# The substitution of a block inversion on GpSimd instead of VectorE, with a planned delay of 41 in place of 36

## The chip, the cores and the metric

One core of a Trainium2 chip runs the whole program. The metric is the device time of one execution in microseconds (us); the kernel before has a median of 1866.65 us over three runs (1861.1 to 1870.76). The engines in this text: PE is TensorE (matmul), PEld its weight loads, DVE is VectorE, ACT is ScalarE, POOL is GpSimd, and SP is SyncE, which here only issues DMAs. Each engine works its own queue in order; semaphores tie the queues together.

## The reference

One decoder layer for a prompt of 1024 tokens and 8 samples of 8 tokens, width 1024. A normalized input goes through one wide projection; its columns feed a sliding-window attention (branch A) and an RWKV-7 recurrence (branch B); both branches are gated, projected, merged and projected once more. The change concerns branch B alone:

```python
def step(S, inp):
    rt, wt, kt, vt, at, bt = inp
    sa = jnp.einsum('bhvk,bhk->bhv', S, at)
    S = S * wt[:, :, None, :] + sa[..., None] * bt[:, :, None, :] + vt[..., None] * kt[:, :, None, :]
    return S, jnp.einsum('bhvk,bhk->bhv', S, rt)
```

This runs over the tokens for 16 heads of 64 by 64 state.

## The kernel before

The recurrence is not computed token by token. The tokens are cut into chunks of 64, and within a chunk the effect of the earlier tokens on the later ones is a triangular system whose matrix is inverted. Sixteen blocks, numbered s = 0 to 15, cover it: s is 4 times the head pair group p (0 to 3) plus the quarter q (0 to 3) of the sequence. A block holds eight such matrices (two pairs of heads, four chunks c), and each block with q = 3 has a second, smaller set for the samples. That makes 20 inversions.

A block goes through these steps. `prep` and `front` (L588) form the arrays and the score matrices: matmuls into PSUM tiles A, which ACT (L803) and DVE (L801) copy to `ab`. `invert` (L833) takes the diagonal blocks of 16 by 16: SP writes `ab` to DRAM (s1, L842) and reads it back with one small matrix per partition (TM, L848); then 15 steps of forward substitution follow, each a multiply into Tt (L854) and an addition into TR (L856), both of 8 to 36 elements per partition and each needing the one before; SP writes TR to DRAM (s2, L858). `merge` (L861) reads the inverses back into `dinv` (L875, half of it issued on SP and half on POOL), transposes them on DVE (L878) and joins the blocks to 64 by 64 by four groups of small matmuls on PE (tiles q_a to q_d). The result is `ti`. `chain` (L921) carries the state through the four chunks of the block. For each chunk: POOL prepares sp, the decayed state (L946); PE forms px; DVE copies it to xs (L954); PE applies ti (tile c, from xs and ti); DVE copies to vsu (L959); PE forms pn; DVE adds sp and pn to the next state in vsu (L970). The chain of block s starts from the state of block s − 1 and needs ti of block s, so the merge of a block must be done by the time that the chain of the block before it ends. `posts` normalizes and gates the output (POOL L1038, L1044, L1045, and the DMA of L1046).

What sets the order: on PE alone the order of this stage is written out by a planner, `drive` (L142). It keeps a clock of planned PE time (`clk`), to which every matmul adds a fixed cost, and eight streams: chains, merges, fronts, preps, samples, posts and the dense projections. A stream says with each `yield` from when it may go on, as a mark plus a delay. The merge of block s waits for the mark `f{s}`, set behind the scores and the inversion, plus WI (L865): the time that the plan allows for the way from the scores to dinv. Where no other stream is due, dense matmuls of the projections (tile d, with weights split into whi and wlo) fill in.

The queues of DVE, ACT, POOL and SP are ordered by a scheduler from priorities and its own estimates: chains and merges have 400000 (`CHAIN`), the inversions 150000 (`INV`, L609), the rest 200000 or 0. So the engine of an instruction also changes where others stand.

POOL has besides the splitting of the weights (L171, 128x1024), the token shift of the projections (L407, L414), the weight DMAs (L169) and the spill DMAs (L426).

Of the kernel before, what the change touches and what calls it, by code (L numbers as in the profile page):

```python
# [12 lines left out]
ALU = mybir.AluOpType  # L13
# [24 lines left out]
MAN = {mybir.EngineType.PE, mybir.EngineType.SP, mybir.EngineType.Pool}  # L38
WX = 0.06
YPR = (200000, 0, 0)  # L40
WI, WD, WB, WA, WM, WH, WS, WP, WT, WR, WE = 36.0, 5.0, 6.0, 2.5, 5.0, 2.0, 3.0, 6.0, 10.0, 4.0, 14.0


T_LORA = 0
# [37 lines left out]
class Prog:  # L82
# [750 lines left out]
    def invert(self, nm, ab, n0, nn):  # L833


        nc, ep = self.nc, self.ep
        nb = 8 * nn
        np_ = 2 * nb
        s1 = self.dp.tile([4 * nn, 32, 32], F32, name=f"s1{nm}")
        s2 = self.dp.tile([2, 4, nn, 16, 16], F32, name=f"s2{nm}")  # L840
        for g in range(4):
            nc.sync.dma_start(s1[g * nn:g * nn + nn].rearrange("n j t -> j n t"), ab[32 * g:32 * g + 32, n0:n0 + nn, 32 * (g % 2):32 * (g % 2) + 32])  # L842
        M = ep.tile([P, 16, 16], F32, tag="TM", name=f"TM{nm}", bufs=1)
        R = ep.tile([P, 8, 16], F32, tag="TR", name=f"TR{nm}", bufs=1)
        tmp = ep.tile([P, 64], F32, tag="Tt", name=f"Tt{nm}", bufs=1)
        for a in range(2):
            for k in range(2):
                nc.sync.dma_start(M[nb * a:nb * a + nb].rearrange("(b k) j t -> k b j t", k=2)[k], s1[:, 16 * a:16 * a + 16, 16 * a:16 * a + 16])  # L848
        nc.sync.dma_start(R[:np_], self.I["ri"][:np_].rearrange("p (a b) -> p a b", a=8))
        for s in range(15):  # L850
            w = 15 - s
            cc = s // 2 + 1
            tv = tmp[:np_, :cc * w].rearrange("p (c t) -> p c t", c=cc)
            nc.vector.tensor_tensor(tv, M[:np_, s:s + 1, s + 1:16].to_broadcast([np_, cc, w]),  # L854
                                    R[:np_, 0:cc, s:s + 1].to_broadcast([np_, cc, w]), ALU.mult)
            nc.vector.tensor_tensor(R[:np_, 0:cc, s + 1:16], R[:np_, 0:cc, s + 1:16], tv, ALU.add)  # L856
        for k in range(2):
            nc.sync.dma_start(s2.rearrange("a g n (c k) t -> k (a g n) c t", k=2)[k], R[:np_].rearrange("(b k) c t -> k b c t", k=2)[k])  # L858
        return s2
# [739 lines left out]
```

## Time and profile before

| | |
|---|---|
| median of 3 runs | 1866.65 us (1861.1 to 1870.76) |
| the profiled execution | 1864.38 us |
| its span | 1862.6 us |
| mean granted PE clock | 0.949 |
| busy: PE, DVE, ACT, POOL | 1686.4, 1139.5, 932.9, 618.0 us |
| stages | start 0 to 190, recurrence 190 to 1300, attention and output to 1863 us |

Busy times say how long an engine worked, not whether anyone waited for it. A wait in the trace is idle time of an engine, put down to what ended it. The granted clock is a share of PE's full speed: 1.00 is the upper of its two levels and 0.5 the lower, so a mean of 0.94 is a mixture of the two. "c" is the PSUM tile of the chain, "d" that of the dense projections.

### The profile page before, as it was taken

Reading aid. Unit: us, or ns where it says so; the run is one execution under the profiler, and the core shown is the slowest. Engines: PE = TensorE matmul, PEld = TensorE weight load, DVE = VectorE, ACT = ScalarE, POOL = GpSimd, SP = SyncE. Lnnn points to the kernel's source line nnn. Section 1 sums busy time; section 2 is a strip of 40 time slices with the busy share of each in tenths; the row PEclk is TensorE's granted clock in tenths of the full one; section 3 lists DMA queues with packets and bytes.
Section 4 is the critical chain, followed back from the end, with each engine's and each line's share of the span. In section 5 each row is a group of like instructions: output and inputs, shape, how many; then the busy total and the mean of one; then the engine's idle time right before and its main releaser. Section 6 shows DMA issues by size and latency. Waiting matters only on the chain. (4 is left out here: it accounts for less than half of the span.)

```text
span 1862.6 us, 37492 instructions
## 1 busy us (share of the span) xinstructions
PE 1686.4 (91%) x13792; PEld 1584.5 (85%) x13792; DVE 1139.5 (61%) x3224; ACT 932.9 (50%) x2353; POOL 618.0 (33%) x872
## 2 busy tenths in 40 slices
PE   5899889888888989889888899999999999999997
PEld 4799888887787878778888888899999899899997
DVE  5323667866777676787676578642366776544443
ACT  5444555444445556555545565434466765432233
POOL 5466444444442653445463343344200000000000
PEclk8899999898898999999999899999999999999999
DMA  4234433333333334334333343223612344364531
GB/s 159 103 126 128 110 97 95 99 97 88 90 97 103 103 93 115 99 101 112 91 105 97 102 136 89 73 90 101 196 60 66 122 130 149 114 221 133 181 109 60
DMA packets 233687, 206.90 MB, mean 111 GB/s; under 512 B 135904, under 2 KB 202608, under 8 KB 233472
## 3 DMA queue, kind: packets, MB, share of 16 engines
q1 hardware_dynamic: 214624, 149.33, 28.0%
q0 software_dynamic: 18880, 55.17, 9.3%
q8 instruction: 109, 1.79, 0.4%
q14 instruction: 74, 0.61, 0.1%
HBM read 140.42 MB, written 65.98 MB: 111 GB/s over the span
## 5 line engine op out<-in xcount | busy, mean ns | idle before, releaser
L110 PE MATMUL d<-hhi,whi 128*128 128x364 f32 (+1 forms) x1656 | 585.7, 354 | 28.6 <-ACT zz L406 9.5
L110 PE MATMUL d<-hlo,whi 128*128 128x364 f32 (+1 forms) x1656 | 568.2, 343 | 11.0 <-DVE hlo L352 8.3
L110 PEld LDWEIGHTS d<-hhi,whi 128*128 128x128 f32 x1656 | 329.6, 199 | 36.5 <-ACT zz L406 10.7
L110 PEld LDWEIGHTS d<-hlo,whi 128*128 128x128 f32 x1656 | 329.5, 199 | 21.0 <-DVE hlo L352 13.0
L110 PE MATMUL d<-hhi,wlo 128*128 128x364 f32 (+1 forms) x1656 | 340.7, 343 | 0.0
L110 PEld LDWEIGHTS d<-hhi,wlo 128*128 128x128 f32 x1656 | 286.5, 196 | 3.4 <-issue 2.4
L171 POOL TENSOR_TENSOR wlo<-wraw,whi 128x1024 fp32r<-128x1024 f32 x56 | 134.3, 2398 | 144.8 <-PE d L110 53.4
L170 ACT ACTIVATE whi<-wraw 128x1024 fp32r<-128x1024 f32 x90 | 94.9, 1055 | 72.8 <-PE d L110 50.7
L1434 POOL TENSOR_TENSOR xr<-xr,frs 128x256 f32<-128x256 f32 x2 | 1.8, 932 | 344.7 <-ACT frs L1431 344.7
L407 POOL TENSOR_TENSOR zz<-zz,pad 128x364 f32<-128x364 f32 (+1 forms) x75 | 71.9, 959 | 116.0 <-ACT pad L404 54.6
L946 POOL TENSOR_TENSOR sp<-vsu,pc 64x128 f32<-64x128 f32 x128 | 57.2, 446 | 125.1 <-DVE vsu L970 115.8
L970 DVE SCALAR_TENSOR_TENSOR vsu<-c,pc,sp 64x64 f32<-64x64 f32 x240 | 67.9, 283 | 41.1 <-PE c L110 37.9
L854 DVE TENSOR_TENSOR Tt<-TM,TR 128x30 f32<-128x30 f32 (+3 forms) x300 | 81.8, 273 | 17.6 <-DMA TM<-s 8.5
L856 DVE TENSOR_TENSOR TR<-TR,Tt 128x30 f32<-128x30 f32 (+3 forms) x300 | 87.3, 291 | 7.1
L1173 ACT ACTIVATE sc<-sc,st 128x256 f32<-128x256 f32 (+1 forms) x128 | 61.8, 484 | 24.5 <-DVE st L1169 24.4
L405 ACT ACTIVATE pad<-d,prm 128x364 f32<-128x364 f32 (+1 forms) x75 | 40.6, 541 | 57.4 <-PE d L110 57.1
L110 PE MATMUL c<-vsu,kbt 128*128 128x128 f32 x256 | 43.1, 292 | 26.0 <-DVE vsu L959 25.9
L1084 POOL TENSOR_TENSOR ylo<-ys,yhi 128x364 fp32r<-128x364 f32 (+1 forms) x6 | 6.5, 1078 | 178.0 <-ACT yhi L1083 178.0
L110 PE MATMUL d<-yhi,whi 128*128 128x364 f32 (+1 forms) x192 | 64.7, 337 | 0.6 <-DVE mb L1354 0.6
L110 PEld LDWEIGHTS c<-vsu,kbt 128*128 128x128 f32 x256 | 36.6, 196 | 33.4 <-DVE vsu L959 32.6
L110 PE MATMUL d<-ol,whi 128*128 128x364 f32 (+1 forms) x192 | 63.1, 329 | 1.5 <-DVE ol L230 1.5
L110 PE MATMUL d<-oh,whi 128*128 128x364 f32 (+1 forms) x192 | 63.3, 330 | 1.2 <-ACT oh L229 1.2
(362 smaller groups left out, 3883.5 us busy)
## 6 DMA issues: line engine op xcount, KB each, us to landing
wraw<-in_w POOLq DMA_DIRECT2D x56, 512.0 KB, 4.2
wraw<-in_w SPq DMA_DIRECT2D x37, 512.0 KB
d_z<-zz POOLq DMA_DIRECT2D x48, 182.0 KB, 2.4
zv<-d_z SPq DMA_DIRECT2D x48, 128.0 KB
w<-d_c SPq DMA_DIRECT2D x24, 256.0 KB
d_m<-sp SPq DMA_DIRECT2D x32, 182.0 KB
stageo<-d_o SPq DMA_DIRECT2D x8, 544.0 KB
d_z<-zz POOLq DMA_DIRECT2D x24, 180.0 KB, 3.8
```

The costliest lines, as they stand in the source:

```text
L110: self.nc.tensor.matmul(out, lhsT=lhsT, rhs=rhs, **kw)
L170: nc.scalar.activation(hi, raw, AF.Copy)
L171: (nc.vector if self.dve_lo else nc.gpsimd).tensor_tensor(lo, raw, hi.bitcast(F32), ALU.subtract)
L405: nc.scalar.activation(pad[:, 1:1 + m], ps[:, :m], AF.Copy, scale=mu)
L407: nc.gpsimd.tensor_tensor(z[:, :m], z[:, :m], pad[:, 0:m], ALU.add)
L854: nc.vector.tensor_tensor(tv, M[:np_, s:s + 1, s + 1:16].to_broadcast([np_, cc, w]), R[:np_, 0:cc, s:s + 1].to_broadcast([np_, cc, w]), AL ...
L856: nc.vector.tensor_tensor(R[:np_, 0:cc, s + 1:16], R[:np_, 0:cc, s + 1:16], tv, ALU.add)
L946: nc.gpsimd.tensor_tensor(sp[h], vsu[h, c, :, h], pc[h, c].unsqueeze(2).to_broadcast([64, 2, HD]), ALU.mult)
L970: nc.vector.scalar_tensor_tensor(dst, pn[h, i, h], pc[h, c, i:i + 1], sp[h, i], ALU.mult, ALU.add)
L1084: (self.nc.gpsimd if kt % 4 == 3 else self.nc.vector).tensor_tensor(lo, t, hi.bitcast(F32), ALU.subtract)
L1173: nc.scalar.activation(sc[k], sc[k], AF.Exp, bias=st[:, 0, k:k + 1], accum_out=st[:, 1, k:k + 1])
L1434: en.tensor_tensor(xt[:, dt, :n], xt[:, dt, :n], rst[:, :n], ALU.mult)
```

## The change

The two operations of each substitution step go from DVE's queue to POOL's, and WI from 36 to 41. Nothing is added or left out.

```diff
--- before.py
+++ after.py
@@ -38,7 +38,7 @@
 MAN = {mybir.EngineType.PE, mybir.EngineType.SP, mybir.EngineType.Pool}
 WX = 0.06
 YPR = (200000, 0, 0)
-WI, WD, WB, WA, WM, WH, WS, WP, WT, WR, WE = 36.0, 5.0, 6.0, 2.5, 5.0, 2.0, 3.0, 6.0, 10.0, 4.0, 14.0
+WI, WD, WB, WA, WM, WH, WS, WP, WT, WR, WE = 41.0, 5.0, 6.0, 2.5, 5.0, 2.0, 3.0, 6.0, 10.0, 4.0, 14.0
 
 
 T_LORA = 0
@@ -851,9 +851,9 @@
             w = 15 - s
             cc = s // 2 + 1
             tv = tmp[:np_, :cc * w].rearrange("p (c t) -> p c t", c=cc)
-            nc.vector.tensor_tensor(tv, M[:np_, s:s + 1, s + 1:16].to_broadcast([np_, cc, w]),
+            nc.gpsimd.tensor_tensor(tv, M[:np_, s:s + 1, s + 1:16].to_broadcast([np_, cc, w]),
                                     R[:np_, 0:cc, s:s + 1].to_broadcast([np_, cc, w]), ALU.mult)
-            nc.vector.tensor_tensor(R[:np_, 0:cc, s + 1:16], R[:np_, 0:cc, s + 1:16], tv, ALU.add)
+            nc.gpsimd.tensor_tensor(R[:np_, 0:cc, s + 1:16], R[:np_, 0:cc, s + 1:16], tv, ALU.add)
         for k in range(2):
             nc.sync.dma_start(s2.rearrange("a g n (c k) t -> k (a g n) c t", k=2)[k], R[:np_].rearrange("(b k) c t -> k b c t", k=2)[k])
         return s2
```

What follows are pieces of the queues at block 8 (pair 2, quarter 0); the chain that runs beside its inversion is that of block 7 (pair 1, quarter 3), and c_32 is its chunk 2. The numbers at the ends of names count buffers and differ between the two kernels.

DVE before, from the last steps of the inversion of block 8 to its transpose L878:

```order
L959 COPY vsu_3_7257<-c_32_8695 64x2x64 x2
L854 TENSOR_TENSOR Tt_00_8431<-TM_00_8429,TR_00_8430 128x8
L856 TENSOR_TENSOR TR_00_8430<-TR_00_8430,Tt_00_8431 128x8
L970 SCALAR_TENSOR_TENSOR vsu_3_7257<-c_32_8695,pc_3_7258,sp_32_8697 64x64 x4
L1005 COPY vss_3_7267<-ss_c 64x64 x2
L1013 TENSOR_TENSOR ve_8833<-vss_3_7267,rco 128x512
L1010 TENSOR_TENSOR ras_3_7269<-ss_y,sx_8718 64x64 x2
L762 SCALAR_TENSOR_TENSOR X_743<-kkn_1_8240,Pp_1_8363 64x4x64
L954 COPY xs_33_8797<-c_33_8796 64x128 x2
L761 TENSOR_TENSOR X_743<-zr_1_8246,Pp_1_8363 64x4x64 x2
L878 STREAM_TRANSPOSE dt_0_8901<-dinv 128x256
```

The transpose stands behind vsu and the state of chunk 2 (its xs is further up) and behind xs of chunk 3.

DVE after, around the same transpose:

```order
L970 SCALAR_TENSOR_TENSOR vsu_3_7393<-c_31_8716,pc_3_7394,sp_31_8718 64x64 x4
L878 STREAM_TRANSPOSE dt_0_9061<-dinv 128x256
L954 COPY xs_32_8883<-c_32_8882 64x128 x2
L1005 COPY vss_3_7403<-ss_c 64x64 x2
L1013 TENSOR_TENSOR ve_8985<-vss_3_7403,rco 128x512
L959 COPY vsu_3_7393<-c_32_8882 64x2x64 x2
L746 TENSOR_TENSOR zk_1_8439<-bo_1_8951,zv_1_8752 128x256
L411 TENSOR_SCALAR pad_728_9049<-shp,prm 128x8
L970 SCALAR_TENSOR_TENSOR vsu_3_7393<-c_32_8882,pc_3_7394,sp_32_8884 64x64 x4
```

It stands right behind the state of chunk 1 (L970 of c_31) and ahead of xs, vsu and the state of chunk 2.

POOL before, from sp of chunk 1 to the DMAs of dinv of block 8:

```order
L946 TENSOR_TENSOR sp_31_8554<-vsu_3_7257,pc_3_7258 64x128 x2
L1038 TENSOR_TENSOR ysb_21_7384<-ysb_21_7384,gn_2_8275 128x256
L1044 TENSOR_TENSOR ysb_21_7384<-ysb_21_7384,bt_2_8589 128x256
L1045 TENSOR_TENSOR ysb_21_7384<-ysb_21_7384,gt_2_8590 128x256
L1046 DMA d_y_70<-ysb_21_7384 128x256
L946 TENSOR_TENSOR sp_32_8697<-vsu_3_7257,pc_3_7258 64x128 x2
L875 DMA dinv<-s_00_8424 16x8x16
L946 TENSOR_TENSOR sp_33_8798<-vsu_3_7257,pc_3_7258 64x128 x2
L875 DMA dinv<-s_00_8424 16x8x16 x3
```

No step of the inversion is here, and sp of chunk 1 stands between the weight DMA and the output of a block.

POOL after, from the middle of the inversion of block 8 to the DMAs of dinv:

```order
L854 TENSOR_TENSOR Tt_00_8497<-TM_00_8495,TR_00_8496 128x35
L856 TENSOR_TENSOR TR_00_8496<-TR_00_8496,Tt_00_8497 128x5x7
L854 TENSOR_TENSOR Tt_00_8497<-TM_00_8495,TR_00_8496 128x30
L946 TENSOR_TENSOR sp_31_8718<-vsu_3_7393,pc_3_7394 64x128 x2
L856 TENSOR_TENSOR TR_00_8496<-TR_00_8496,Tt_00_8497 128x5x6
...
L856 TENSOR_TENSOR TR_00_8496<-TR_00_8496,Tt_00_8497 128x8
L1038 TENSOR_TENSOR ysb_21_7509<-ysb_21_7509,gn_2_8289 128x256
L1044 TENSOR_TENSOR ysb_21_7509<-ysb_21_7509,bt_2_8787 128x256
L875 DMA dinv<-s_00_8490 16x8x16 x4
```

The pair of sp of chunk 1 stands behind 19 of the 30 steps, and two operations of the output stand between the last step and the DMAs of dinv.

## Rows read from the trace of the kernel before

**Rows 1.** The page: busy us, share of the span, number of instructions.

```profile
PE 1686.4 (91%) x13792; PEld 1584.5 (85%) x13792; DVE 1139.5 (61%) x3224; ACT 932.9 (50%) x2353; POOL 618.0 (33%) x872
```

**Rows 2.** Window of the stage: us, engines' busy us (number), PE's clock, DMA share, GB/s.

```profile
190.00:1300.00 1110.00, 983.88 (x9246) 922.21 (x9245) 759.48 (x2212) 580.73 (x1498) 494.18 (x714) 0.94 0.36 99
```

**Rows 3.** PE's waits, 190 to 1300: us in total, times, longest us.

```profile
PE c L110 <- DVE vsu L959: 25.9, 19, 4.4
PE c L110 <- DVE xs L954: 15.5, 9, 3.2
PE lo L110 <- DVE X L809: 11.4, 7, 3.1
```

**Rows 4.** Windows in which an inversion runs, two of them and the sum.

```profile
686.80:702.00 15.20, 9.39 (x45) 9.08 (x44) 14.25 (x54) 7.82 (x23) 4.59 (x11) 0.78 0.46 151
735.50:750.30 14.80, 13.75 (x118) 13.28 (x117) 13.87 (x56) 9.38 (x27) 3.27 (x6) 1.00 0.36 110
...
sum 299.50, PE 239.05 PEld 227.84 DVE 279.80 ACT 160.05 POOL 126.87; mean PE 11.95 PEld 11.39 DVE 13.99 ACT 8.00 POOL 6.34
```

**Rows 5.** The page's groups: busy us, mean ns of one; idle us before them.

```profile
L854 DVE TENSOR_TENSOR Tt<-TM,TR 128x30 f32<-128x30 f32 (+3 forms) x300 | 81.8, 273 | 17.6 <-DMA TM<-s 8.5
L856 DVE TENSOR_TENSOR TR<-TR,Tt 128x30 f32<-128x30 f32 (+3 forms) x300 | 87.3, 291 | 7.1
```

**Rows 6.** Windows of the stage's rest, the last and the sum.

```profile
1215.90:1300.00 84.10, 84.10 (x752) 80.77 (x751) 27.36 (x74) 38.03 (x85) 38.95 (x49) 0.99 0.28 91
sum 810.50, PE 744.83 PEld 694.37 DVE 479.68 ACT 420.67 POOL 367.31; mean PE 35.47 PEld 33.07 DVE 22.84 ACT 20.03 POOL 17.49
```

**Rows 7.** Two POOL lines: ns of one operation, smallest/median/largest, and when.

```profile
L414 POOL TENSOR_TENSOR zz<-zz,pad x25: 301/322/709, 75.5 to 976.5; 128x64 f32<-128x64 f32 x25
...
L322 POOL TENSOR_TENSOR acc<-acc,sq x12: 940/1052/1822, 14.4 to 34.0; 128x364 f32<-128x364 f32 x6, 128x360 f32<-128x360 f32 x6
```

**Rows 8.** POOL's timeline: start us, length us, what it does.

```profile
29.02 6.86 POOL L322 TENSOR_TENSOR acc<-acc,sq 128x360 f32<-128x360 f32 x6
...
743.07 0.94 POOL L946 TENSOR_TENSOR sp<-vsu,pc 64x128 f32<-64x128 f32 x2 [3.00 <-DVE vsu L970]
```

**Rows 9.** DVE's timeline at block 8, [idle us before, who ended it].

```profile
739.87 0.18 DVE L854 TENSOR_TENSOR Tt<-TM,TR 128x36 f32<-128x36 f32 x1
...
746.33 0.58 DVE L954 COPY xs<-c 64x128 f32<-64x128 f32 x2
...
750.14 0.17 DVE L856 TENSOR_TENSOR TR<-TR,Tt 128x8 f32<-128x8 f32 x1
...
760.04 0.45 DVE L878 STREAM_TRANSPOSE dt<-dinv 128x256 f32<-128x256 f32 x1 [2.46 <-DMA dinv<-s]
```

**Rows 10.** PE's timeline at the same place.

```profile
743.07 0.83 PE L110 MATMUL d<-hhi,wlo 128*128 128x364 f32 x4
743.73 0.61 PE L110 MATMUL c<-vsu,X 128*128 128x128 f32 x4
...
747.88 0.55 PE L110 MATMUL c<-xs,ti 128*128 128x64 f32 x4
```

**Rows 11.** DVE's timeline at blocks 1 and 13.

```profile
265.26 1.18 DVE L970 SCALAR_TENSOR_TENSOR vsu<-c,pc,sp 64x64 f32<-64x64 f32 x4
...
272.84 0.45 DVE L878 STREAM_TRANSPOSE dt<-dinv 128x256 f32<-128x256 f32 x1 [0.74 <-DMA dinv<-s]
...
1093.47 1.16 DVE L970 SCALAR_TENSOR_TENSOR vsu<-c,pc,sp 64x64 f32<-64x64 f32 x4
...
1097.73 0.45 DVE L878 STREAM_TRANSPOSE dt<-dinv 128x256 f32<-128x256 f32 x1 [0.29 <-DMA dinv<-s]
```

**Rows 12.** DVE's waits, 190 to 1300.

```profile
DVE dt L878 <- DMA dinv<-s: 16.9, 11, 3.3
```

**Rows 13.** POOL's waits, 190 to 1300.

```profile
POOL sp L946 <- DVE vsu L970: 115.8, 35, 15.6
```

## The prediction

> **What bounds the kernel now.** The busy shares come first: VectorE (DVE) works 61% of the span, GpSimd (POOL) 33% [rows 1]. The split by stage says where the change can act. All 20 inversions lie between 190 and 1300 us, in the recurrent stage; there PE works 983.88 of 1110 us and is idle for 126.1 us, at a granted clock of 0.94 [rows 2]. Dense projection work is at hand all through that stage, but PE's order is fixed beforehand, so PE idles whenever the next instruction of that order misses an operand. PE's waits name the operands: chain matmuls wait for DVE's copies (vsu of L959 25.9 us, xs of L954 15.5 us), others for DVE's X (11.4 us) [rows 3]. The stage is bound by PE, plus what DVE delivers late.
>
> Idle costs more than itself. A clock of 0.94 between the levels 2.4 and 1.2 GHz puts (1 − 0.94) × 2 = 12% of 1110 us, 133 us, at the lower one; half of it, 67 us, is lost work, 67/126.1 = 0.53 us for each idle us. It goes with stalls: of two inversions, one with 5.81 us of idle PE shows 0.78, one with 1.05 us shows 1.00 [rows 4]. I count an idle us as 1.53 us.
>
> **What goes.** DVE loses 300 multiplies (81.8 us) and 300 adds (87.3 us) [rows 5]. Only what PE waited for counts. In the 20 stretches in which an inversion runs, 299.5 us from each first L854 to its last L856, PE is busy 239.05 us: idle 60.45 us, 20.2% [rows 4]. In the rest of the stage it is idle 810.5 − 744.83 = 65.67 us, 8.1% [rows 6]. If DVE, rid of the inversion, brings these stretches to the share of the rest, 60.45 − 0.081 × 299.5 = 36 us of idle go. I take that gain whole.
>
> **What a run costs on POOL.** The trace has no such operation there. The mean one has 372/15 = 24.8 elements per partition. The nearest row from above is L414's addition of 64, median 0.322 us; L322, of about 362, has 1.052 us; their line is 2.45 ns per element and gives 0.226 us at 24.8 [rows 7]. Each step needs the one before: six L322 in a row take 6.86 us, 1.143 each, so about 0.09 us lies between two [rows 8]. Thirty take 30 × 0.226 = 6.8 us (no pause) to 30 × (0.322 + 0.09) = 12.4 us. I take 0.25 + 0.09, nearer the line since it is at the size asked for: 10.2 us. Between them the new order of POOL has other operations, a mean of 2.7 us per run at their durations of before (in block 8 the pair of sp_31): 12.9 us. Before, a run took 299.5/20 = 15.0 us, since other work of DVE lay between. So the result is ready about 2.1 us sooner. The way from there is as long as it was: in block 8 the last step ended at 750.31 and the transpose, held by dinv alone, started at 760.04 [rows 9].
>
> **What moves: the transpose on DVE.** DVE works its queue in order. L878 waits for dinv, and whatever stands behind it waits too. In block 8 the queue of before has L878 behind the xs, the vsu and the state of chain step 32; in that of after it stands right behind the state of step 31, ahead of all three. A scheduler that no longer has 30 steps on DVE puts L878 earlier; the data doesn't follow. The copy xs_32 ran at 746.33 and the transpose at 760.04: what now stands behind it ran 13.7 us ahead of it [rows 9]. In block 1 the state that now stands behind it ran at 265.26 and the transpose at 272.84, 7.6 us; in block 13 it is 1093.47 and 1097.73, 4.3 us [rows 11]. From block 1 to block 13, the 12 blocks where the two can be compared have leads of 3.2 to 13.7 us, mean 7.3 (12, 14 and 15 change their place in the plan too far, 0 has no chain ahead).
>
> From that lead several things go. The delay of 41 for 36 sets q_a some 24 dense matmuls further behind its block's scores, but the chain moves along: counted in PE's planned order, the copy in question stands a mean of 9 further behind (28 in block 8, none in block 2). Four start at 743.07 and the next instruction at 743.73, 0.165 us each [rows 10]: 1.5 us. The data is ready 2.1 us sooner. And PE has something in hand before it needs the copy: xs_32 was done at 746.91 and used at 747.88, 0.97 us; on a free DVE it would have been done at about 745.0, as its matmuls end at 744.34, which makes 2.9 us [rows 9, 10]; I take 1.9. What is added: L878 itself, 0.45, and 36/16 = 2.3 us by which the chain now reaches its copy sooner, since it no longer loses the 36 us, while the inversion does not. That is 7.3 − 1.5 − 2.1 − 1.9 + 0.45 + 2.3 = 4.55 us per block. Some of it is there already: DVE waits at L878 for 16.9 us before [rows 12], 1.1 a block, and I count half of that as idle that PE has now. 4.0 us for each of 15 blocks: 60 us of new idle.
>
> **The sum.** 60 − 36 = 24 us of idle, × 1.53 = 37 us: the profiled 1864.4 becomes 1901. The median shown, 1866.65, is 2.3 us above that execution: 1904 us. The longer delay by itself I cost at nothing: what it lets pass is dense work that is to be done anyway, and at the end of the stage, from 1215.9 to 1300, PE is busy for 84.10 of 84.10 us [rows 6], enough for the last chain steps to slip into. Without that cover the slip would show in full: the last q_a stands 120 dense matmuls later, 20 us.
>
> Ends of the unknown cost: with 6.8 us for a run the data comes 3.4 us sooner still, 0.6 us per block, 9 − 36 = −27 us of idle, −41 us: 1826. With 12.4 us it comes 2.2 us later, 6.2 us per block, 93 − 36 = 57, +87 us: 1954.
>
> **Rivals.** *DVE's relief decides.* The stall behind L878 is met by what stands ready on PE, or POOL's run is at its lower end. For it: DVE's copies are PE's largest waits, and L878 waits in the trace of before too without being one. Against it: the copies that now stand behind L878 are the very ones that PE waits for. Time: −36 × 1.53 = −55 us at most, 1812; with a third given back, 1830. Chance 0.23.
>
> *A wash.* 36 us go and 30 to 42 come: 1857 to 1876. Chance 0.15.
>
> *POOL late.* The other side of the relief: sp (L946), which L970 needs, and the additions of the projections queue on POOL among or behind the steps; in block 8 sp_31 stands behind 19 of the 30. For it: POOL could take sp the moment that vsu came, and waited 115.8 us for that in all [rows 13]; now it is in the middle of a run. Against it: sp_32 was done at 744.01, and its L970 came behind the step of 750.14, over 6 us later [rows 8, 9]. It decides from the point where a run keeps a sp for longer than that; 3 us of it in 10 of the 20 runs would be 30 × 1.53 = +46 us on top of the sum, 1950. Chance 0.10.
>
> *Dear steps.* An operation at the upper end, 0.412 us with its pause: 1954 as above. Against it: L414 is two and a half times as large as the mean step and takes 0.322 us. Chance 0.08. The Trainium skill speaks for it, in "GPSIMD Engine Reference", section 8 (Key points): for elementwise work DVE is structurally about twice as fast. By that rule a step would cost an estimated 2 × 0.18 = 0.36 us (L854 at 36 elements took 0.18 on DVE [rows 9]), 0.45 with the pause, and a run 13.5 us, 1.1 us beyond my upper end, which would give 1.1 × 15 × 1.53 = 25 us more, 1979; the trace agrees only in part, L414's 0.322 us at 64 elements being less than that.
>
> That the change doesn't do what it says can be left out: the new order of POOL has the 30 steps.
>
> **How the numbers follow.** The sum as worked out, 1904, has 0.44 (its own range 1877 to 1940), POOL late 0.10, dear steps 0.08, the wash 0.15, the relief 0.23. A measurement of this kernel tells about 0.5%, 9.3 us, from no change: faster is below 1857 and slower above 1876, which gives 0.23, 0.15 and 0.62. The range that is to hold 8 in 10 takes in the wash, the nearer part of the relief and POOL late: 1840 to 1955.
>
> **What would show it.** Right: DVE waits for dinv at L878 for 50 us or more in place of 16.9, with L954, L959 or L970 right behind; PE's waits for vsu and xs grow and the clock of the stage falls below 0.94; a run takes 10 to 15 us on POOL. Wrong: PE is idle for less than 126 us in the stage, a run takes under 9 us with what lies between, or L878 finds dinv already there. That DVE's two-input work or sp wait on POOL instead would show in the waits on POOL's releases.

## The result, and the profile after

The changed kernel has a median of 1911.41 us (1901.23 to 1915.92, 4 runs) against 1865.24 us of the kernel before: a ratio of 1.0242, 95% interval 1.0204 to 1.0280, slower by some 45 us. The profiled execution has a span of 1909.4 us, 46.8 more than before, at a mean granted clock of 0.933 (0.949 before); in the recurrent stage alone it is 0.92, where it was 0.94 [rows 2].

The busy times of the page after (us, share of the span, instructions) show what moved: DVE 136 us down, POOL 160 us up, PE 10.5 us up for the same 13792 matmuls.

```profile
PE 1696.9 (89%) x13792; PEld 1599.0 (84%) x13792; DVE 1003.4 (53%) x2624; ACT 930.5 (49%) x2353; POOL 777.6 (41%) x1472
```

The stage is longer now: its last inversion ends at 1278.1, so the windows reach to 1363, 85 us behind it as before. The first sum is over the 20 windows in which an inversion runs, the second over the rest (engines' busy us).

```profile
sum 263.50, PE 242.55 PEld 235.96 DVE 147.84 ACT 151.39 POOL 216.44; mean PE 12.13 PEld 11.80 DVE 7.39 ACT 7.57 POOL 10.82
sum 909.50, PE 762.22 PEld 710.30 DVE 476.75 ACT 432.53 POOL 439.23; mean PE 36.30 PEld 33.82 DVE 22.70 ACT 20.60 POOL 20.92
```

Beside the inversions PE idles 263.50 − 242.55 = 21.0 us, where it was 60.45 [rows 4]; in the rest it idles 909.50 − 762.22 = 147.3 us, where it was 65.67 [rows 6]. So 39 us of idle went and 82 came. A run takes 263.50/20 = 13.2 us instead of 15.0.

DVE's wait at the transpose and ACT's wait for POOL, both from 190 us to 1363 (us in total, times, longest us), are the two that grew most:

```profile
DVE dt L878 <- DMA dinv<-s: 83.0, 12, 10.2
```

```profile
ACT ysb L1039 <- POOL ysb L1038: 104.3, 31, 10.6
```

The first was 16.9 us [rows 12]; the second was 43.4 us in the trace of before. DVE's timeline at block 1 (start us, length us, and in brackets the idle time and what ended it) shows the first in the place that rows 11 show of before:

```profile
263.39 0.29 DVE L959 COPY vsu<-c 64x128 f32<-64x128 f32 x1
271.72 0.45 DVE L878 STREAM_TRANSPOSE dt<-dinv 128x256 f32<-128x256 f32 x1 [8.04 <-DMA dinv<-s]
272.18 1.20 DVE L970 SCALAR_TENSOR_TENSOR vsu<-c,pc,sp 64x64 f32<-64x64 f32 x4
```

The matmuls that L970 needs end at 265.8, so it stands ready behind the transpose for some 6 of the 8.04 us. Block 9 has PE's longest idle piece at a transpose, DVE's lines first and PE's next:

```profile
846.04 0.45 DVE L878 STREAM_TRANSPOSE dt<-dinv 128x256 f32<-128x256 f32 x1 [9.22 <-DMA dinv<-s]
846.41 0.57 DVE L959 COPY vsu<-c 64x128 f32<-64x128 f32 x2
```

```profile
847.03 1.22 PE L110 MATMUL c<-vsu,kbt 128*128 128x128 f32 x4 [10.74 <-DVE vsu L959]
```

PE's pieces of idle time that end between 0.5 us ahead of a transpose's start and 4.5 us behind its end add up to 54 us over the 16 blocks; before it was 9 us. One piece of the 54, 8.6 us at block 3, is not the transpose's: L878 does not wait for dinv there, and PE waits for ACT. So 45 us lie at the other transposes.

PE's waits for the chain's copies, from 190 us to 1363, grew by less (they were 25.9 and 15.5 us [rows 3]), and a wait for ACT's L831 came up that was absent before:

```profile
PE c L110 <- DVE vsu L959: 32.9, 12, 10.7
PE c L110 <- DVE xs L954: 17.4, 5, 11.2
PE t_34k L108 <- ACT vsu L831: 13.8, 3, 7.4
PE lo L110 <- ACT vss L831: 8.6, 1, 8.6
```

Block 8, the place that the prediction showed, does not show the transpose's wait. There L878 finds dinv already landed, since DVE had been held earlier, by a chain through POOL and ACT. The three timelines, POOL's, ACT's and DVE's, in this order:

```profile
760.30 0.21 POOL L856 TENSOR_TENSOR TR<-TR,Tt 128x8 f32<-128x8 f32 x1
760.46 0.72 POOL L1038 TENSOR_TENSOR ysb<-ysb,gn 128x256 f32<-128x256 f32 x1
```

```profile
754.63 0.40 ACT L713 ACTIVATE kkn<-kkn 128x256 f32<-128x256 f32 x1
761.21 0.60 ACT L1039 ACTIVATE ysb<-ysb,prm 128x256 f32<-128x256 f32 x1 [6.18 <-POOL ysb L1038]
761.72 0.40 ACT L714 ACTIVATE kkn<-kkn 128x256 f32<-128x256 f32 x1
```

```profile
754.95 0.95 DVE L731 TENSOR_TENSOR KB<-e,sg 64x256 f32<-64x256 f32 x2
762.15 0.74 DVE L715 SCALAR_TENSOR_TENSOR kkn<-zk,prm,kkn 128x256 f32<-128x256 f32 x1 [6.25 <-ACT kkn L714]
769.11 0.45 DVE L878 STREAM_TRANSPOSE dt<-dinv 128x256 f32<-128x256 f32 x1
```

L1038 stands behind the last of the 30 steps; its input was there at 754.4, when ACT ended L1037. ACT's L1039 waits for it with its whole queue, L714 among it, and DVE's L715 waits for L714. One late multiply idles two engines for 6 us. This is a second path by which the steps can cost time, and the prediction had not seen it. It reaches PE: each of the four waits for ACT's L831 above, 22.4 us together, ends 1.1 to 1.8 us behind the start of an L1039 that had itself waited 4.5 to 9.1 us for L1038. What the path is worth in time, the experiments leave open.

### The profile page after: what moved, and what is told of

Read it like the earlier page. It is cut to its first block, busy times and chain, and to the rows that moved or that the text cites. A ratio compares the mean times of both kernels' runs of the same rounds, so it can differ in the third digit from the quotient of the medians.

```text
span 1909.4 us, 37510 instructions
## 1 busy us (share of the span) xinstructions
PE 1696.9 (89%) x13792; PEld 1599.0 (84%) x13792; DVE 1003.4 (53%) x2624; ACT 930.5 (49%) x2353; POOL 777.6 (41%) x1472
## 4 chain that ended last, share of the span: by engine, by line
PE 54%; POOL 15%; DMA 9%; issue 7%; DVE 6%; ACT 4%; SPq 2%; POOLq 0%; DVEq 0%; ACTq 0%
PE d L110 32%; PE wo L110 5%; POOL Tt L854 4%; POOL TR L856 4%; PE c L110 3%; PE s L110 2%; PE o L110 2%; DMA s<-TR 2%; PE A L110 2%; PE y L110 2%; POOL wlo L171 2%; PE pt L108 1%; DMA zk<-d_z 1%; DMA dinv<-s 1%; POOL dinv L875 1%
## 5 line engine op out<-in xcount | busy, mean ns | idle before, releaser
L110 PE MATMUL d<-hhi,wlo 128*128 128x364 f32 (+1 forms) x1656 | 345.7, 348 | 0.0
L110 PEld LDWEIGHTS d<-hhi,wlo 128*128 128x128 f32 x1656 | 292.7, 200 | 2.7 <-issue 1.7
L407 POOL TENSOR_TENSOR zz<-zz,pad 128x364 f32<-128x364 f32 (+1 forms) x75 | 69.8, 932 | 96.4 <-ACT pad L404 37.7
L854 POOL TENSOR_TENSOR Tt<-TM,TR 128x30 f32<-128x30 f32 (+3 forms) x300 | 83.2, 277 | 42.3 <-DMA TM<-s 20.0
L970 DVE SCALAR_TENSOR_TENSOR vsu<-c,pc,sp 64x64 f32<-64x64 f32 x240 | 67.9, 283 | 47.3 <-PE c L110 44.0
L856 POOL TENSOR_TENSOR TR<-TR,Tt 128x30 f32<-128x30 f32 (+3 forms) x300 | 81.4, 271 | 21.7
L731 DVE TENSOR_TENSOR KB<-e,sg 64x256 f32<-64x256 f32 x128 | 71.1, 570 | 6.2 <-issue 4.9
L1039 ACT ACTIVATE ysb<-ysb,prm 128x256 f32<-128x256 f32 (+1 forms) x32 | 19.7, 614 | 105.2 <-POOL ysb L1038 105.2
```

The lines of the kernel that those rows point to most:

```text
L110: self.nc.tensor.matmul(out, lhsT=lhsT, rhs=rhs, **kw)
L407: nc.gpsimd.tensor_tensor(z[:, :m], z[:, :m], pad[:, 0:m], ALU.add)
L731: nc.vector.tensor_tensor(KB[hr, :4, j, :], self.v64(t)[hr], self.d64(Pi, 1)[hr], ALU.mult)
L854: nc.gpsimd.tensor_tensor(tv, M[:np_, s:s + 1, s + 1:16].to_broadcast([np_, cc, w]), R[:np_, 0:cc, s:s + 1].to_broadcast([np_, cc, w]), AL ...
L856: nc.gpsimd.tensor_tensor(R[:np_, 0:cc, s + 1:16], R[:np_, 0:cc, s + 1:16], tv, ALU.add)
L970: nc.vector.scalar_tensor_tensor(dst, pn[h, i, h], pc[h, c, i:i + 1], sp[h, i], ALU.mult, ALU.add)
```

## The experiments

Ratios are to the kernel before, run beside it on the same chip, with 95% intervals; 1% is 18.6 us.

**Holding the transpose.** In the changed kernel, L878 gets something to follow: a small matmul, which PE's planned order sets 10 planned us ahead of q_a, and a copy of one column of its result.

```diff
-        yield f"f{s}", WI
+        yield f"f{s}", WI - 10.0, "t"
...
+        pz = self.ps("t", f"z{nm}")
+        self.mm(pz[0:32, 0:32], lhsT=self.cst(C_ID, 32, 0, 32), rhs=self.cst(C_ID, 32, 0, 32), start=True, stop=True)
+        nc.vector.tensor_copy(dt[0:32, 0, 0:1], pz[0:32, 0:1])
         nc.vector.transpose(flat(dt), flat(D))
-        yield None, 0.0, "t"
+        yield None, 10.0, "t"
```

> Steps on GpSimd, delay 41, as in the changed kernel; only the place of the transpose L878 on VectorE differs: a 32x32 matmul that PE's planned order sets 10 planned us ahead of q_a feeds a one-column copy into dt, which L878 has to follow, so L878 stands on average at chain operation 86.1 as in the kernel before, not at 83.6. Transpose theory: VectorE's wait for dinv falls from 83 us to under 20; PE's stalls just at L878 (54 us after, 9 before) go, 45 x 1.53 = 69 us, so about 1842 us. Rival, output operations on GpSimd behind the steps hold ScalarE (L1039, 102 us of waiting against 42): that wait stays and the time falls by 10 us at most, about 1900 us.

Measured: 1.0056 (1.0033 to 1.0080), 35 us below the changed kernel, give or take 8. The wait for dinv at the transpose is all but gone from DVE's list, and PE's idle time, from 190 us to 85 us behind the last inversion, falls from 168.2 to 142.3 us. But ACT still waits as long (its lines are numbered three higher here):

```profile
ACT ysb L1042 <- POOL ysb L1041: 101.0, 31, 12.0
```

So the transpose's place is worth about half of what my theory gave it (69 us), and the rest is elsewhere. Neither theory had the number.

**Taking L1038 off POOL.**

```diff
-        nc.gpsimd.tensor_tensor(y, y, rs, ALU.mult)
+        nc.vector.tensor_tensor(y, y, rs, ALU.mult)
```

> As the changed kernel, but the multiply of L1038 (31 operations, normalization of the output) goes back from GpSimd to VectorE, so that ScalarE's L1039 no longer waits for an operation behind the 30 steps; L878 stands where it stands in the changed kernel. ScalarE theory: L1039's wait falls from 102 us to under 30 and the time by about 40 us, to 1870. Transpose theory: L878 still waits for some 80 us and the time stays within 10 us of 1911, less at most what ScalarE's wait adds.

Measured: 1.0160 (1.0120 to 1.0200), 15 us below the changed kernel on the scale of the ratios. ACT's wait fell to 33.6 us, but DVE's at the transpose rose: what ACT no longer delayed, the transpose did.

```profile
DVE dt L878 <- DMA dinv<-s: 99.8, 14, 9.9
```

So taking away one wait of 70 us gives 15. That two queues hold the same work in turn would explain it, but is not shown; that the gains of e1 and e2 add up in e5 below speaks against it.

**Each part of the change alone.** The steps on POOL with the old delay, and the new delay with the steps on DVE.

```diff
-WI, WD, WB, ... = 41.0, 5.0, 6.0, ...
+WI, WD, WB, ... = 36.0, 5.0, 6.0, ...
```

> The steps on GpSimd alone, with the delay of 36 as before. L878 stands at chain operation 85.0 on average (83.6 with 41, 86.1 before). Transpose theory: VectorE's wait for dinv about 60 us, time between, about 1885 to 1895 us. Rival, the longer delay is what costs: back to 1866 us. Rival, the longer delay helps as PE waits less for q_a: slower than 1911 us.

> The delay of 41 alone, the steps on VectorE. Transpose theory and the prediction: the longer delay by itself costs nothing, within 10 us of 1866; L878 stands at 85.3 on average, slightly earlier than before (86.1), which may add a few us. Rival, the delay is what costs: 1890 us or more.

Measured: steps on POOL at 36 are 1.0253 (1.0211 to 1.0295), as slow as at 41, and the steps on DVE at 41 are 0.9885 (0.9842 to 0.9928), faster than before by some 21 us. Both expectations failed. The longer delay is a gain where the steps are on DVE: PE's idle time in the stage falls from 126 to 116 us and its waits for vsu from 25.9 to 16.9. With the steps on POOL it gives nothing. So the steps on POOL cost 0.025 at a delay of 36 and 0.036, 66 us, at 41. In e3 the wait for dinv was 73.4 us and the time as in the changed kernel, so the time does not follow that wait alone.

**Both causes taken away, and more off POOL.** e5 has the hold and L1038 on DVE; e6 also has the additions of the token shift there.

```diff
-            nc.gpsimd.tensor_tensor(z[:, :m], z[:, :m], pad[:, 0:m], ALU.add)
+            nc.vector.tensor_tensor(z[:, :m], z[:, :m], pad[:, 0:m], ALU.add)
...
-                nc.gpsimd.tensor_tensor(zs, zs, smp[:, :, 0:8], ALU.add)
+                nc.vector.tensor_tensor(zs, zs, smp[:, :, 0:8], ALU.add)
```

> Steps on GpSimd, delay 41, the transpose held at its place as in e1, and L1038 on VectorE as in e2. If the transpose (35 us in e1) and ScalarE's wait behind the steps (17 us in e2) are two separate costs, they add: 1911 - 52 = about 1859 us, PE's idle time from 190 us on about 125 us. Rival, they are one queue of delays: no better than 1877 us.

> As e5, and the additions of the token shift (L407, L414, 75 and 25 operations) go from GpSimd to VectorE too, so that neither ScalarE nor VectorE waits for them behind the steps; VectorE's L411 and L402 waited 65 us in e1 for L407's result. If other work behind the steps on GpSimd is what still costs: about 1845 us, level with the steps on VectorE at a delay of 41 (1842). Rival, VectorE is again too full (some 35 us more work in this stage): 1859 us or above.

Measured: e5 0.9982 (0.9959 to 1.0005), 1857.58 us where 1859 was expected; e6 0.9858 (0.9821 to 0.9896), 1838.20 us. The parts add up: 0.0186 and 0.0082 apart, 0.0260 together. With e6 the steps on POOL seemed to cost nothing any more; the control below took that back.

**Controls with the steps on DVE.** The hold alone, the delay at 46, and the moves of e6, each on the kernel of e4.

> The steps on VectorE, delay 41, the transpose held as in e1: what the hold does by itself. VectorE waits 28 us for dinv in e4 and PE stalls 5.9 us at it, so at best 6 to 10 us less than 1842: 1832 to 1842 us. Rival, that the added matmul and copy or the other place of the transpose cost by themselves: 1850 us or more, and then e1 understates what the transpose costs.

> The steps on VectorE with a delay of 46. If the longer delay helps because PE reaches chain and merge with their operands ready, 46 gives a little more or as much as 41: 1830 to 1845 us. Rival, the transpose theory also without GpSimd: L878 stands at 84.25 on average (85.3 with 41, 86.1 before, 83.6 in the changed kernel), waits for dinv for 40 us or more, and the gain is given back: 1850 to 1865 us.

> Control for e5 and e6: the steps on VectorE with a delay of 41, and L1038, L407 and L414 on VectorE as in e6. If what e5 and e6 removed was work that stands behind the steps on GpSimd, the moves give nothing here, where no steps stand there, and VectorE is some 50 us fuller: 1842 to 1865 us. Rival, these operations are better on VectorE whatever the steps do: 1825 us or below.

Measured: e7 0.9899 (0.9865 to 0.9932), no different from e4 and 2 us above the range that was expected. What the hold gives in e1 is thus the place of the transpose. But DVE's wait for dinv fell from 28.0 to 2.6 us in e7 without a gain, so the hold may cost by itself the 6 to 10 us that were expected of it, and e1 may understate the transpose by as much. With the transpose held on both sides, e1 against e7, the steps on POOL still cost 0.0157, 29 us. e8 1.0078 (1.0050 to 1.0107): 46 gives the gain of 41 back and more, but not by the way expected, as L878 waited for dinv for only 17.9 us there; why is open. e9 0.9742 (0.9697 to 0.9787), 1816.39 us: the rival held. L1038, L407 and L414 are better on DVE even where no steps stand on POOL, worth 0.0143, 27 us; the three were not parted. In its trace DVE works more and waits for POOL not at all (25.3 us in e4). So of the 0.0198 from e1 to e6 most is not a price of the steps. 0.0055, 10 us, is left for it; the interval of that difference, about 0.008 to either side, holds zero, so this part is not shown.

e9 is the fastest kernel of the study, 2.6% below the kernel before: the inversion stays on DVE, the delay is 41, and the work that ACT and DVE wait for leaves POOL.

**Is the transpose still a cost without the late output work, and what is left?** e10 is e6 without the hold; e11 is e6 with a delay of 36; e12 is e6 with sp on DVE.

> As e6 without the hold: steps on GpSimd, delay 41, L1038, L407 and L414 on VectorE, and the transpose where the changed kernel has it (83.6). If the transpose's place costs by itself, VectorE waits 80 us or more for dinv and the time is 35 us above e6, about 1873 us. Rival, the two causes were one, and without the late GpSimd work the transpose costs nothing: within 10 us of 1838 us.

> As e6 with a delay of 36 in place of 41. In e6 q_a came 7.7 to 19 us behind the transpose, so the result is there in time at 36 too: if the delay only has to cover the way, 1830 to 1845 us. Rival, the delay of 41 by itself is worth what it is with the steps on VectorE (23 us): about 1860 us.

```diff
-                nc.gpsimd.tensor_tensor(sp[h], vsu[h, c, :, h], pc[h, c]...
+                nc.vector.tensor_tensor(sp[h], vsu[h, c, :, h], pc[h, c]...
```

> As e6, and sp (L946, 128 operations) goes from GpSimd to VectorE. In e6 VectorE's copy into vsu waits 31.5 us in 16 cases for sp, which reads vsu and stands among the steps on GpSimd, and PE waits 31.2 us for that copy; with the steps on VectorE (e9) the first wait is absent and the second 10.6 us. If that is what is left of the price of the steps on GpSimd: about 1816 us, level with e9. Rival, the 36 us more work on VectorE and the way back from GpSimd keep it: 1835 us or more.

Measured: e10 1.0098 (1.0059 to 1.0138), 0.0240 or 45 us above e6, with a wait for dinv of 106.3 us. The place of the transpose is a cost by itself. e11 1.0039 (1.0018 to 1.0061): at 36 the gain is lost, 0.018 or 34 us where the rival had 23, though no matmul of PE waits for dt. It need not be the delay alone: the held transpose waits for its data again, which in e6 it did for 1.6 us.

```profile
DVE dt L881 <- DMA dinv<-s: 29.7, 8, 6.7
```

e12 0.9828 (0.9785 to 0.9872): its interval overlaps e6's. What it set out to take away it did, first e6, PE's wait for the copy, and DVE's wait for sp, which reads vsu:

```profile
PE c L110 <- DVE vsu L962: 31.2, 13, 7.3
```

```profile
DVE vsu L962 <- POOL sp L949: 31.5, 16, 5.1
```

then e12, where the second line is absent and the first reads

```profile
PE c L110 <- DVE vsu L962: 9.9, 9, 2.6
```

but PE's idle time stayed (120.2 and 119.5 us): other waits took its place, 9.7 us at q_3b and 9.4 at q_3a among them. 0.0116, 22 us, between e6 and e9 remain of the steps' price; it is not settled by what.

## Why the prediction was right

It named 1904 us, slower with a chance of 0.62; the time is 1911. The mechanism held: the inversion's own stalls went, and the transpose moved ahead of the chain's copies and held them. Three of its sizes did not hold, partly in opposite directions, so that the time came out so near is in part luck.

- **What goes.** 36 us of idle beside the inversions were forecast to go; 39 went.
- **What a run costs.** 0.34 us a step and 12.9 us a run were forecast. The spread of the multiply on POOL (ns: smallest, median, largest) has a median of 0.241 us:

```profile
L854 POOL TENSOR_TENSOR Tt<-TM,TR x300: 195/241/849, 206.7 to 1277.6; 128x30 f32<-128x30 f32 x24, 128x14 f32<-128x14 f32 x16, 128x24 f32<-128x24 f32 x16, 128x15 f32<-128x15 f32 x8
```

 Most steps of block 8 start 0.28 to 0.33 us apart where nothing lies between, some 0.38 to 0.77, and a run took 13.2 us. The line through L414 and L322 (0.226) was the right row to read. The rule that I weighed, from the Trainium skill, "GPSIMD Engine Reference", section 8 (Key points), would have had an estimated 0.36; here POOL took 1.3 times DVE's 0.183 us (median in the trace of before) at this size, and the dear steps fall as a rival. By the mean of one multiply the two are even equal within 2%, 273 ns on DVE [rows 5] and 277 on POOL:

```profile
L854 POOL TENSOR_TENSOR Tt<-TM,TR 128x30 f32<-128x30 f32 (+3 forms) x300 | 83.2, 277 | 42.3 <-DMA TM<-s 20.0
```

- **The transpose.** L878 did stand ahead of the chain's copies and did wait, 83.0 us. Its cost in PE's idle time was put at 60 us. At the transposes PE's stalls grew by 36 us (block 3 left out), and holding the transpose took 26 us of idle and 35 us of time away (e1), 32 and 45 in e10 against e6. The mechanism is right, the term nearly twice too large. The block that was shown for it is one of four where something else was later.
- **POOL late.** It was a rival with 0.10 and not in the sum, and the trace shows it as well, though on another path: L1038 behind the steps holds ACT, and PE waits 22.4 us for what stands behind it on ACT. sp among the steps holds little in the changed kernel; once the transpose is held, it holds the copy L959, which overwrites what sp reads, rather than L970 (31.5 us in e6). What this is worth in time is not shown: e5, e6 and their control leave 10 us, which is not clear of zero, and a part of the 22 us that stay open.
- **The longer delay.** This step failed. The prediction costed it at nothing, as what it lets pass is dense work that the end of the stage covers. On the kernel before it gains 21 us (e4), and the steps on POOL take it back: the change is −0.0115 for the delay and +0.0357 for the steps. I had looked at whether the work that the delay lets pass is lost, not at what reaching the chain later does to PE's waits.
- **An idle us at 1.53.** Idle grew by 42 us (126.1 to 168.2) where 24 were forecast, and the span by 46.8, so 1.11 here. Over the 14 profiled kernels of this study a straight line through span against idle has a slope of 1.38. A price of 1.53 on too small a number came out near the truth by two errors that cancelled: 24 × 1.53 = 37, 42 × 1.11 = 47. The 24 were right in part by luck too: 60 us of new idle were all to come from the transpose, and of the 82 that came it accounts for 26 to 36; the rest came by paths that the sum did not have.

## What to carry to other kernels

When work leaves an in-order queue, look at what the scheduler puts in its place: an instruction that waits for a long way round (here two trips through DRAM) moves up as soon as the queue looks free, and blocks what was ahead of it. Give it something to follow that comes late enough. Before moving work to an idle engine, ask who waits for the short operations already there: an idle engine that answers at once is worth something, and 30 dependent steps in its queue take that away (ACT's wait for L1038 went from 43.4 to 104.3 us). Here it paid to move those short operations off it and leave the long work where it was. Change a planned delay by itself, too: here it gained 21 us where the move that it came with lost 66.

## What the runs showed that I had not expected

The delay of 41 makes the kernel 1.15% faster than 36, and 46 makes it 0.78% slower (e4, e8), and I found no wait in the traces that explains both; the plan's order matters at this level, by ways that stay open. And taking a wait away often moves it: e2 took 71 us from ACT's wait for L1038 and DVE's wait for dinv rose by 17; e12 took 21 us from one wait of PE and its idle time stayed within 1 us.
